# Following each batch read of sample states with one adaLN unit in a hybrid GLA and Mamba-2 decoder step

## The chip, the cores and the metric

The kernel runs on one core of a Trainium2 chip. The metric is the device time of one execution in microseconds: 2923.5 us, the median of three runs (2923.2 to 2926.08).

## The reference

One decoder layer for 256 prompt tokens and 8 sequences of 8 sample tokens (320 token columns), in float32. The vector `c` of each sequence gives six adaLN parts of 2048 values; they scale, shift and gate the two halves of the layer.

```
mod  = silu(c) @ w_ada + b_ada                 # 9 rows of c; w_ada is 2048 x 12288
h    = rmsnorm(x) * (1 + sc1) + sh1
proj = h @ w_in
# GLA, 4 heads:  S_t = diag(a_t) S_{t-1} + k_t^T v_t ,  o_t = q_t S_t
# SSD, 64 heads in 8 groups:  h_t = exp(dt_t A) h_{t-1} + dt_t x_t B_t^T ,  y_t = h_t C_t
x = x + g1 * ((sigmoid(gA) * yA + sigmoid(gB) * yB) @ w_mix_out)
x = x + g2 * SwiGLU(rmsnorm(x) * (1 + sc2) + sh2)
y = rmsnorm(x) * final_norm
```

The sample sequences start from stored states (8 sequences x 4 heads x 256 x 512 for GLA; 8 x 64 heads x 64 x 128 for SSD), which are read, updated and written back.

## The kernel before

**Weights.** All large products run as "quads": `quad_mm` (L318) takes a 512 x 512 block of a weight matrix in two halves. A half is one transfer of 128 x 1024 float32 (524,288 bytes) into a buffer with the tag `raw`, of which there are four (`load_raw`, L160). ScalarE casts it to `whi` and VectorE makes the rest `wlo` (`split_w`); of these pairs there are three. TensorE then runs 24 matmuls of 128 x 320 per half (`block`, L312: three per 128 x 128 tile). `Stream.ahead` (L190) asks for the half two further on each time the first of a half's four column blocks is done. TensorE's order is that of the program; the other engines and SyncE's queue (SP), which issues every transfer, are ordered by the compiler's scheduler, in program order as far as buffers and data allow. `now(...)` says that a transfer is placed no earlier in that order than the TensorE instruction before it.

**adaLN units.** `class Ada` (L242) cuts `w_ada` into units. A unit of the later kind is a 128 x 2048 block: two raw transfers (`load`, L253) and four matmuls with 32 columns of stationary each, put side by side in TensorE at column positions 0, 32, 64 and 96 (`mm`, L275); in float32 they run as eight passes. After each fourth unit the sums are copied out (`adap`, L291), and at the next call of `mm` the `flush` (L294) transposes that copy (four matmuls `p`) and writes the strips of `mod`. 96 units there are; 64 are left when the GLA part starts, and four of them are kept for the end of the mixing stage. Between, `gemm` (L352) puts one unit into each quad whose number divides by `ada_every`: its load at the start of the quad, its matmuls at the end. `ada_every` is 0 through the GLA heads and 2 from L926 to the end of the units, so 60 units go there.

**States.** Beside the quads runs a background: `bg.tick()` is called after each of a quad's eight column blocks (a tick is six matmuls), and a generator's `yield n` lets n ticks pass, so that it goes on at the one after those. `gla_work` (L640) and `ssd_work` (L963) handle the sample states as 128 x 512 tiles (262,144 bytes, ten buffers). `States.read` (L617) loads ahead to tile 4n + 8 and then runs four matmuls of the same shape as an adaLN unit, 32 columns each at positions 0 to 96, as eight passes named `inter`. `States.update` (L624) runs one matmul `upd`, changes one tile and stores the one before. A GLA head has four reads, an SSD group two: 32 in all. In a GLA head the first read comes at tick 18 of the head's work (24 in the first head) and the others each 10 ticks later; in an SSD group at ticks 16 and 26. Behind the first read of an SSD group two tiles `csb` of 655,360 bytes each are loaded (L1003). `bg.drain()` runs what is left of the background at once, with no quads beside it; the first head has eight quads, 64 ticks, before it.

Of the kernel before, what the change touches and what calls it, by code (L numbers as in the profile page):

```python
# [60 lines left out]
def hybrid_kernel(tc, ctx, a, o):  # L61
# [186 lines left out]
    class Ada:  # L248
# [12 lines left out]
        def load(self, small=False, spare=False):  # L261
            if self.units:
# [8 lines left out]
                    raws = [load_raw(src[:, h * 1024:(h + 1) * 1024], spare or c < 8) for h in range(2)]  # L271
                self.loaded.append((c, b0, nb, q, raws))

        def mm(self):
            self.flush()  # L275
            if not self.loaded:
                return
            c, b0, nb, q, raws = self.loaded.pop(0)
            if q == 0:
                t = psum.tile([128, 512], F32, tag="ad", bufs=1, name="ad")  # L280
                self.ps = t
            w = 128 * nb
            m = 2048 // w
            n = m // len(raws)
            for j in range(m):
                T.matmul(self.ps[32 * (j % 4):32 * (j % 4) + 32, :w], c_s[:, m * q + j, :],
                         raws[j // n][:, (j % n) * w:(j % n) * w + w], start=q == 0 and j < 4,
                         stop=q == nb - 1 and j >= m - 4, tile_position=(0, 32 * (j % 4)))
            if q == nb - 1:
                part = stile([128, 512], name="adap")  # L290
                S.copy(part[:, :w], self.ps[:, :w])  # L291
                self.parts.append((c, b0, nb, part))
# [59 lines left out]
    def gemm(names, quads, evac, apart=False):  # L352
        pss = [mm_ps() for _ in range(4)]
        n = len(names)
        for q in range(n):
            quad_no[0] += 1
            xq = quads(q) if callable(quads) else quads[q]
            quad_mm(pss, names[q], xq, q == 0, q == n - 1, evac,
                    1 if ada_every[0] and len(ada.units) > 4 and quad_no[0] % ada_every[0] == 0 else 0, apart,
                    (lambda: quads(q + 1)) if callable(quads) and q + 1 < n else None)  # L360


# [149 lines left out]
    def stack_k(ps, hf, n):  # L512

        R = pool.tile([96, n, 128], F32R, tag="k", bufs=3, name="R")
        src = ps[quarter(hf), 0:128 * n].rearrange("p (a b) -> p a b", a=n)
        S.copy(R[quarter(0)], src)
        S.copy(R[quarter(1)], src)
        tt(V, R[quarter(2)], src, R[quarter(hf)].bitcast(F32), ALU.subtract)
        return [stack_stationary(R[:, i]) for i in range(n)]
# [120 lines left out]
    def gla_work(H):  # L640
        hd, vT, KK, qe, kx = H.hd, H.vT, H.KK, H.qe, H.kx
        order = [(4 * hf + j, kb) for hf in range(2) for kb in range(2) for j in range(4)]
        states = States([a["S_gla"][hd, b, kb] for b, kb in order], [o["gla_s"][hd, b, kb] for b, kb in order])
        yield 6 if hd else 12
        states.load(4)
        yield 4


        psK = ax_ps("kT")
        for kb in range(2):  # L650
            T.transpose(psK[0:64, 128 * kb:128 * kb + 128], kx[:, kb, 0:64], ident)
        ps = ax_ps("vT")
        for mb in range(4):
            T.transpose(ps[0:64, 128 * mb:128 * mb + 128], vT[:, mb, NP:], ident)
        S.copy(xs_tok[0:64], ps[0:64])
        hst = [stack_k(psK, hf, 2) for hf in range(2)]
        yield 4

        psA = ax_ps("inter")
        for n in range(4):  # L660
            hf, kb = divmod(n, 2)
            if kb == 0:
                mv = stack_v(xs_tok, hf)
            states.read(psA, [H.qpad[:, kb, 4 * hf + j] for j in range(4)], n, n == 0, n == 3)
            yield 1
            for j in range(4):
                tok = NP + 8 * (4 * hf + j) + 7

                def decay(st, ps, kb=kb, tok=tok):
                    V.scalar_tensor_tensor(out=st, in0=st, scalar=H.eb[:, kb, tok:tok + 1], in1=ps,  # L670
                                           op0=ALU.mult, op1=ALU.add)

                states.update(n, j, hst[hf][kb][:, j], mv, decay)
                yield 1
        inter = stile([128, 512], name="inter")
        S.copy(inter, psA)
        yield 1
        states.store(16)
        vt = []
        for tb in range(2):  # L680
            ps = ax_ps("vT")
            for mb in range(4):
                T.transpose(ps[:, 128 * mb:128 * mb + 128], vT[:, mb, 128 * tb:128 * tb + 128], ident)
            v = stile([128, 512], name="vtok")
            S.copy(v, ps)
            vt.append(v)
            yield

        att = stile([128, 448], name="att")
        now(G.memset(att, 0.0))  # L690
        ps = ax_ps("att")
        for i in range(4):
            for kb in range(2):
                T.matmul(ps[:, 64 * i:64 * i + 64], KK[kb][:, 256 * i:256 * i + 128],
                         qe[:, kb, 64 * i:64 * i + 64], start=kb == 0, stop=kb == 1)
        yield
        for i in (2, 3):
            for kb in range(2):
                T.matmul(ps[:, 128 + 64 * i:192 + 64 * i], KK[kb][:, 256 * i + 128:256 * i + 256],
                         qe[:, kb, 64 * i:64 * i + 64], start=kb == 0, stop=kb == 1)  # L700
        for kb in range(2):
            T.matmul(ps[0:64, 384:448], H.kes[:, kb], qe[:, kb, NP:], start=kb == 0, stop=kb == 1)
        V.copy_predicated(att[:, 0:384], mask[:, 0:384].bitcast(I32), ps[:, 0:384])
        V.copy_predicated(att[0:64, 384:448], mask[0:64, 384:448].bitcast(I32), ps[0:64, 384:448])
        yield

        k4 = stile([128, 2, 256], name="k4")
        for sb in range(2):
            ps = ax_ps("k4")
            for kb in range(2):  # L710
                T.transpose(ps[:, 128 * kb:128 * kb + 128], KK[kb][:, 1024 + 128 * sb:1152 + 128 * sb], ident)
            S.copy(k4[:, sb], ps[:, 0:256])
            yield

        oT = qtile(name="oT")
        ss = ntile([128, NT], name="ss")
        for mb in range(4):
            c = slice(128 * mb, 128 * mb + 128)
            ps = ax_ps("o")
            T.matmul(ps[:, 0:256], vt[0][:, c], att[:, 0:256], start=True, stop=False)  # L720
            T.matmul(ps[:, 128:256], vt[1][:, c], att[:, 256:384], start=False, stop=True)
            T.matmul(ps[:, 256:320], xs_tok[0:64, c], att[0:64, 384:448], start=True, stop=False)
            T.matmul(ps[:, 256:320], inter[:, c], sel, start=False, stop=True)
            S.copy(oT[:, mb], ps[:, :NT])
            sq_acc(ss, oT[:, mb], mb == 0, G)
            yield
        yield 4
        while H.r is None:
            yield
        rs = rstd_from([ss], 512)  # L730
        H.hi = qtile(F32R, name="ohi")
        H.lo = qtile(F32R, name="olo")
        for mb in range(4):
            V.scalar_tensor_tensor(out=oT[:, mb], in0=oT[:, mb], scalar=vec[:, V_GN + mb:V_GN + mb + 1],
                                   in1=rs, op0=ALU.mult, op1=ALU.mult)
            tt(G, oT[:, mb], oT[:, mb], H.r[:, mb], ALU.mult)
            split(H.hi[:, mb], H.lo[:, mb], oT[:, mb])
        for kb in range(2):
            ps = ax_ps("fin")
            for sb in range(2):  # L740
                T.matmul(ps, k4[:, sb, 128 * kb:128 * kb + 128], vt[sb], start=sb == 0, stop=sb == 1)
                yield
            fs = stile([128, 512], name="fs")
            S.copy(fs, ps)
            nc.sync.dma_start(o["gla_p"][hd, kb], fs)
# [177 lines left out]
    prev = heads[3]  # L923


    ada_every[0] = 2  # L926

    def conv_evac(ck, dst, cvs, cvo):
        def f(mb, pss):
# [40 lines left out]
    def ssd_work(W):  # L970
# [19 lines left out]
        xl = stile([64, 512], name="xl")  # L990
        tt(V, v8(xl), v8(ps[0:64]), bc8(dtL_tok[:, hsl]), ALU.mult)
        tt(V, v8(xs_tok[0:64]), v8(ps[0:64]), bc8(dt_tok[0:64, 2, hsl]), ALU.mult)
        yield 4

        psA = ax_ps("inter")
        for hf in range(2):
            mv = stack_v(xl, hf)
            states.read(psA, [cpad[:, 4 * hf + j] for j in range(4)], hf, hf == 0, hf == 1)
            for j in range(4):
                st = states.tiles[4 * hf + j]  # L1000
                tt(G, v8(st), v8(st), bc8(ecs_all[:, hsl, 4 * hf + j]), ALU.mult)
# [8 lines left out]
            yield 1  # L1010
            for j in range(4):
                states.update(hf, j, hst[hf][:, j], mv, lambda st, ps: tt(V, st, st, ps, ALU.add))
                yield 1
        inter = stile([128, 512], name="inter")
        tt(V, v8(inter), v8(psA), bc8(ecs_r[:, hsl]), ALU.mult)
# [418 lines left out]
```

## Time and profile before

| what | value |
|---|---|
| median of three runs | 2923.5 us |
| the profiled execution | 2922.56 us |
| its span, first to last instruction | 2920.8 us |
| mean granted TensorE clock | 0.995 of full speed |
| TensorE busy (matmul) | 2874.5 us, 98% |
| VectorE, ScalarE, GpSimd busy | 54%, 42%, 13% |
| moved by DMA | 575.54 MB, mean 197 GB/s |

In the page, PE is TensorE's matmuls and PEld its weight loads, DVE is VectorE, ACT ScalarE, POOL GpSimd and SP the queue that issues the transfers. The GLA part lies at about 185 to 610 us, the SSD groups at about 610 to 1655 us.

### The profile page before, as it was taken

What the parts mean: (1) busy time and instruction counts of PE and PEld (TensorE: products, weight loads), DVE (VectorE), ACT (ScalarE), POOL (GpSimd) and SP (SyncE); (2) the same over time, 40 slices, a digit from 0 to 9 for tenths busy, and PEclk for the clock granted to TensorE, in tenths of its full rate; (3) what the DMA queues carried; (4) which work ended last, traced back from release to release, by engine and by line L of the source; (5) the groups of instructions that cost most, each with busy time, mean ns of one, the idle gap of its engine ahead of it and who ended that gap; (6) DMA issues with size and microseconds to landing.
All of it is one profiled execution on the core that took longest, in us unless ns stands there. A gap on an engine that the chain in (4) does not pass through costs nothing.

```text
span 2920.8 us, 48446 instructions
## 1 busy us (share of the span) xinstructions
PE 2874.5 (98%) x19596; PEld 2687.3 (92%) x19596; DVE 1584.6 (54%) x2302; ACT 1239.1 (42%) x1954; POOL 375.5 (13%) x517
## 2 busy tenths in 40 slices
PE   7999999999999999999999999999999999999998
PEld 5799788998889889889988999999999999999998
DVE  5666555756656565666565554456434444444445
ACT  4344544343554554545454343335333233323333
POOL 0002121212232232323223000000000000000000
PEclk9999999999999999999999999999999999999998
DMA  9847636657676675775757554454444444444443
GB/s 385 321 146 238 202 126 215 220 177 264 221 245 232 228 254 191 253 237 206 265 194 253 195 170 161 165 211 145 152 151 148 149 152 152 147 149 152 151 147 114
DMA packets 181112, 575.54 MB, mean 197 GB/s; under 512 B 23253, under 2 KB 24601, under 8 KB 180889
## 3 DMA queue, kind: packets, MB, share of 16 engines
q1 hardware_dynamic: 180888, 572.45, 57.5%
q8 instruction: 154, 2.52, 0.3%
q14 instruction: 70, 0.57, 0.1%
HBM read 528.63 MB, written 43.74 MB: 196 GB/s over the span
## 4 chain that ended last, share of the span: by engine, by line
PE 55%; DVE 1%; ACT 0%; issue 0%; DVEq 0%
PE mm L115 52%; PE ad L115 1%; PE y L115 0%; DVE x L106 0%; PE sum L115 0%; PE upd L115 0%; PE fin L115 0%; PE inter L115 0%; DVE x L1182 0%; PE p L118 0%; PE cb L115 0%; PE xT L118 0%; DVE ss L106 0%; DVE wlo L106 0%; DVE yb L106 0%
## 5 line engine op out<-in xcount | busy, mean ns | idle before, releaser
L106 DVE TENSOR_TENSOR wlo<-raw,whi 128x1024 fp32r<-128x1024 f32 x712 | 881.4, 1240 | 933.9 <-ACT whi L132 923.4
L132 ACT CAST whi<-raw 128x1024 fp32r<-128x1024 f32 x712 | 745.8, 1048 | 1384.8 <-PE mm L115 1040.6
L115 PE MATMUL mm<-hh,whi 128*128 128x320 f32 x2560 | 813.2, 318 | 2.4 <-ACT hh L132 2.0
L115 PE MATMUL mm<-hl,whi 128*128 128x320 f32 x2560 | 791.0, 309 | 1.3 <-DVE hl L106 1.3
L115 PE MATMUL mm<-hh,wlo 128*128 128x320 f32 x2560 | 791.7, 309 | 0.1
L115 PEld LDWEIGHTS mm<-hh,whi 128*128 128x128 f32 x2560 | 481.3, 188 | 81.3 <-issue 37.3
L115 PEld LDWEIGHTS mm<-hl,whi 128*128 128x128 f32 x2560 | 481.7, 188 | 10.1 <-issue 2.9
L115 PEld LDWEIGHTS mm<-hh,wlo 128*128 128x128 f32 x2560 | 481.5, 188 | 0.6 <-DVE wlo L106 0.4
L115 PE MATMUL mm<-gh,whi 128*128 128x320 f32 x1408 | 435.3, 309 | 0.8 <-ACT gh L1256 0.8
L115 PE MATMUL mm<-gl,whi 128*128 128x320 f32 x1408 | 435.4, 309 | 0.0
L115 PE MATMUL mm<-gh,wlo 128*128 128x320 f32 x1408 | 435.1, 309 | 0.0
L115 PEld LDWEIGHTS mm<-gh,whi 128*128 128x128 f32 x1408 | 264.3, 188 | 1.8 <-ACT gh L1256 1.8
L115 PEld LDWEIGHTS mm<-gl,whi 128*128 128x128 f32 x1408 | 264.3, 188 | 0.5 <-DVE gl L106 0.3
L115 PEld LDWEIGHTS mm<-gh,wlo 128*128 128x128 f32 x1408 | 264.3, 188 | 0.0
L115 PE MATMUL mm<-ahi,whi 128*128 128x320 f32 x704 | 217.5, 309 | 0.0
L115 PE MATMUL mm<-alo,whi 128*128 128x320 f32 x704 | 217.5, 309 | 0.0
L115 PE MATMUL mm<-ahi,wlo 128*128 128x320 f32 x704 | 217.5, 309 | 0.0
L106 POOL TENSOR_TENSOR ss<-ss,sq 128x320 f32<-128x320 f32 x14 | 12.4, 883 | 1398.0 <-ACT sq L109 1397.9
L115 PE MATMUL mm<-yhi,whi 128*128 128x320 f32 x512 | 170.4, 333 | 0.1
L115 PE MATMUL mm<-yhi,wlo 128*128 128x320 f32 x512 | 158.4, 309 | 0.2 <-DVE wlo L106 0.2
L115 PE MATMUL mm<-ylo,whi 128*128 128x320 f32 x512 | 158.0, 309 | 0.0
L115 PEld LDWEIGHTS mm<-ahi,whi 128*128 128x128 f32 x704 | 132.1, 188 | 0.0
(281 smaller groups left out, 3624.6 us busy)
## 6 DMA issues: line engine op xcount, KB each, us to landing
raw<-w_in SPq DMA_DIRECT2D x320, 512.0 KB, 3.8
raw<-w_fi SPq DMA_DIRECT2D x176, 512.0 KB, 3.6
raw<-w_ada SPq DMA_DIRECT2D x120, 512.0 KB, 5.7
raw<-w_fo SPq DMA_DIRECT2D x88, 512.0 KB, 3.5
raw<-w_sp SPq DMA_DIRECT2D x64, 512.0 KB, 5.0
araw<-w_ada SPq DMA_DIRECT2D x52, 512.0 KB, 8.9
st<-S_gla SPq DMA_DIRECT2D x64, 256.0 KB, 5.1
gla_s<-st SPq DMA_DIRECT2D x64, 256.0 KB, 4.7
```

Of the source, the lines that this page charges most:

```text
L106: return eng.tensor_tensor(out=out, in0=in0, in1=in1, op=op)
L115: Tensor.last = nc.tensor.matmul(*args, **kw)
L132: first = S.copy(hi, src)
```

## The change

Reads and units are coupled. `Ada.unit` is the old `mm` without the flush in front. `Ada.preload` loads one unit if none is waiting. In the background each `states.read` is followed at once by `ada.unit()`, and the next unit's load is issued there or, for the first read, five ticks before it. The flush moves behind the first update after each read. `ada_every` goes from 2 to 4, a quad takes no unit while one is loaded, and the GLA heads' ticks change: the first pause is 2 instead of 6 (not in the first head), and the pause after the first update of each four is 2 instead of 1. So the reads of a GLA head come at ticks 14, 25, 36 and 47 (24, 35, 46 and 57 in the first head).

```diff
+        def preload(self):
+            if len(self.units) > 4 and not self.loaded:
+                self.load()
+
         def mm(self):
             self.flush()
+            self.unit()
+
+        def unit(self):
             if not self.loaded:
                 return
...
-                    1 if ada_every[0] and len(ada.units) > 4 and quad_no[0] % ada_every[0] == 0 else 0, apart,
+                    1 if ada_every[0] and len(ada.units) > 4 and quad_no[0] % ada_every[0] == 0 and not ada.loaded else 0, apart,
...
-        yield 6 if hd else 12
+        yield 2 if hd else 12
...
         hst = [stack_k(psK, hf, 2) for hf in range(2)]
+        ada.preload()
         yield 4
...
             states.read(psA, [H.qpad[:, kb, 4 * hf + j] for j in range(4)], n, n == 0, n == 3)
+            ada.unit()
+            if n < 3:
+                ada.preload()
             yield 1
...
                 states.update(n, j, hst[hf][kb][:, j], mv, decay)
-                yield 1
+                if j == 0:
+                    ada.flush()
+                yield 2 if j == 0 else 1
...
-    ada_every[0] = 2
+    ada_every[0] = 4
...
         tt(V, v8(xs_tok[0:64]), v8(ps[0:64]), bc8(dt_tok[0:64, 2, hsl]), ALU.mult)
+        ada.preload()
         yield 4
...
             states.read(psA, [cpad[:, 4 * hf + j] for j in range(4)], hf, hf == 0, hf == 1)
+            ada.unit()
+            if hf == 0:
+                ada.preload()
...
                 states.update(hf, j, hst[hf][:, j], mv, lambda st, ps: tt(V, st, st, ps, ALU.add))
+                if j == 0:
+                    ada.flush()
                 yield 1
```

## Rows read from the trace of the kernel before

**Rows 1.** The page's first part: busy time and share of each engine.
```profile
PE 2874.5 (98%) x19596; PEld 2687.3 (92%) x19596; DVE 1584.6 (54%) x2302; ACT 1239.1 (42%) x1954; POOL 375.5 (13%) x517
```

**Rows 2.** The chain in order of time: start us, us, what, passes.
```profile
1426.37 1.00 PE inter L115 x8
1427.36 0.86 PE ad L115 x8
1428.22 1.95 PE mm L115 x12
1430.41 1.76 PE mm L115 x12
...
1445.36 0.99 PE ad L115 x8
1446.35 1.95 PE mm L115 x12
...
1532.28 1.00 PE inter L115 x8
1533.27 0.59 PE p L118 x4
1533.86 0.99 PE ad L115 x8
```

**Rows 3.** Groups by line on TensorE, whole span: xcount | busy us, mean ns | idle before.
```profile
L115 PE MATMUL ad<-raw,c_s 128*32 128x512 f32 x480 | 63.8, 604 | 0.0
...
L115 PE MATMUL inter<-st,cpad 128*32 128x512 f32 x128 | 17.0, 605 | 0.0
```

**Rows 4.** Stretches: us, busy of PE PEld DVE ACT POOL, PEclk, DMA share, GB/s.
```profile
640.00:1655.00 1015.00, 1012.49 (x7053) 906.78 (x7051) 635.27 (x910) 498.64 (x932) 289.68 (x398) 1.00 0.68 231
683.00:693.00 10.00, 10.00 (x72) 8.86 (x70) 5.32 (x8) 4.04 (x8) 2.39 (x3) 1.00 0.63 213
693.00:713.00 20.00, 20.00 (x133) 16.41 (x132) 14.05 (x16) 6.35 (x10) 10.30 (x8) 1.00 0.95 341
240.00:274.00 34.00, 34.00 (x227) 29.38 (x225) 21.12 (x22) 12.18 (x15) 2.61 (x3) 1.00 0.88 295
285.00:310.00 25.00, 20.84 (x106) 15.36 (x106) 10.09 (x13) 11.37 (x23) 6.90 (x7) 0.93 0.18 67
```

**Rows 5.** Timeline of the issuing queue in the first SSD group.
```profile
692.44 1.85 SPq L619 DMA_DIRECT2D st<-S_ssm  x4
694.33 1.11 SPq L1008 DMA_DIRECT2D csb<-cs_d  x2
695.54 0.47 SPq L167 DMA_DIRECT2D raw<-w_in  x1
...
700.42 0.38 SPq L167 DMA_DIRECT2D raw<-w_ada  x1
...
701.42 0.51 SPq L167 DMA_DIRECT2D raw<-w_ada  x1
```

**Rows 6.** Timeline: split and first use of a half behind csb, two SSD groups.
```profile
704.86 1.05 ACT L132 CAST whi<-raw 128x1024 fp32r<-128x1024 f32 x1 [7.29 <-DMA raw<-w_in]
705.95 1.53 DVE L106 TENSOR_TENSOR wlo<-raw,whi 128x1024 fp32r<-128x1024 f32 x1 [2.64 <-ACT whi L132]
707.60 0.34 PE L115 MATMUL mm<-hh,wlo 128*128 128x320 f32 x1
...
1057.32 1.23 DVE L106 TENSOR_TENSOR wlo<-raw,whi 128x1024 fp32r<-128x1024 f32 x1 [1.23 <-ACT whi L132]
1060.04 0.31 PE L115 MATMUL mm<-hh,wlo 128*128 128x320 f32 x1
```

**Rows 7.** Timeline: split and first use of a half in the first GLA head.
```profile
255.02 1.23 DVE L106 TENSOR_TENSOR wlo<-raw,whi 128x1024 fp32r<-128x1024 f32 x1
263.37 0.31 PE L115 MATMUL mm<-hh,wlo 128*128 128x320 f32 x1
```

**Rows 8.** The tile ad: the copy on ScalarE, ns min/median/max.
```profile
L291 ACT COPY adap<-ad x26: 372/583/602, 20.9 to 1972.4; 128x512 f32<-128x512 f32 x22, 128x256 f32<-128x256 f32 x4
```

## The prediction

> **What bounds the kernel now.** I began with the page's busy shares: TensorE's matmuls fill 98% of the span and no other engine comes near [rows 1]. A table of stretches confirms it where the change works: in the SSD part, 640 to 1655 us, matmuls are busy 1012.49 of 1015 us at granted clock 1.00, the higher level, 2.4 GHz [rows 4]. So only less TensorE time per piece of work helps there, and the price of every new wait is paid in full.
>
> Next I read the chain in order of time for what a change of shape costs. Twelve steady weight matmuls take 1.76 us; the twelve behind an adaLN unit take 1.95. A unit alone (0.99) with its aftermath (0.19) thus costs 1.18 us, and a read, of the same shape, as much. Where a read and a unit stand together, the chain has 1.00, then 0.86, then 1.95 for twelve: 2.05 us for both, against 2 x 1.18 = 2.36 apart. **A pair saves 0.31 us** [rows 2].
>
> Last I looked at how early weights arrive, in the timelines. In the first GLA head a half's split ends at 256.25 (255.02 + 1.23) and is first used at 263.37, 7.1 us later [rows 7]. In the SSD groups the half whose transfer is issued behind the two csb loads is much tighter: in the first group ScalarE waits 7.29 us for it, the split ends at 707.48 and the first use is at 707.60, 0.1 us later; in another group it is 1058.55 and 1060.04, 1.5 us [rows 6]. I count four groups of the first kind and four of the second. The reserve is small there because the transfers are: the DMA engines are 0.95 busy at 341 GB/s from 693 to 713 us, though only 0.63 in the ten microseconds before [rows 4].
>
> **The change part by part.**
>
> *The pairs.* The 480 passes under `raw` are 60 units of eight, and the 128 passes of `inter` in the SSD groups are 16 reads of eight [rows 3]; the GLA heads have 16 more. Four units go to each GLA head and two to each SSD group, so all 32 reads get one, and 28 units stay in quads. By the ticks every preload finds none waiting: the quad numbers divisible by four are the last of each group of four quads, and the one in an SSD group's z product is left out, since a unit is loaded then. The slots suffice for the 28. Eight of the 32 reads are followed by a unit already: four directly (the last at 1426.37), four with a flush between (the last at 1532.28). The 24 new pairs save 24 x 0.31 = 7.4 us. In the other four the flush moves away: 1.00 + 0.59 + 0.99 + 0.19 = 2.77 becomes 2.05 and a flush of at most 0.59, so 0.13 to 0.31 each; I take 0.22, 0.9 us [rows 2]. Together **-8.3 us**, between -7.9 and -8.6.
>
> *The flushes.* Their number stays; eight of them now come two ticks (some 2 us) after their unit. The copy takes 0.58 us on ScalarE [rows 8], and a cast of 1.05 us [rows 6] can stand ahead of it: 1.6 us, so it fits and I take nothing. If a cast that waits for its weights stands ahead, TensorE waits with it; at 1 us each that would be 8 us, which I keep for the upper end.
>
> *The first GLA head.* Its updates now end at tick 66 of 64, so one falls into the drain. The stretch of that drain has matmuls busy 20.84 of 25 us [rows 4], there is nothing to hide behind. One `upd` and its store: 0.3 us, bounds 0 and 2. **+0.3 us**. The other heads end at the same tick as before (4 earlier at the start, one more for each of four reads).
>
> *Transfers in the GLA heads.* Sixteen units' loads of 1.05 MB move here, three of them in each head between the first read and the last, which lie 33 ticks, some 38 us, apart. The stretch now moves 295 GB/s at a share of 0.88, so 335 at a share of 1 [rows 4]. With the reads 11 ticks apart instead of 10 this thins to 268; three units in 38 us add 83: 351 against 335. That is 5% too much for 38 us, 1.8 us late per head at most if nothing absorbs it, against a reserve of 7.1 [rows 7]. But a waiting unit holds two of the four raw buffers nearly throughout, so the weights run less far ahead, and the next unit's load can block the queue until the present unit has run; behind it stand state loads, stores and weights. Bounds 0 and 7.2 us for four heads; nearest is the reserve, so I take 0.25 per head: **+1.0 us**.
>
> *Transfers in the SSD groups.* This decides. The second unit of a group is now loaded behind the first read (693 us in the first group); before, its two transfers went out at 700.42 and 701.42, behind the csb loads and the weights issued at 695.54 [rows 5]. It comes ahead of them, and its 1.05 MB at 341 GB/s are 3.1 us [rows 4]. Had the queue no room, each tight group would lose 3.0 us and each other 1.6. The room is in the stretch before, 0.37 of 10 us idle [rows 4], enough for 3.7 us; but a load starts only when a raw buffer comes free, and the order of the buffers lets one of the two transfers go early (the weights' half that stood behind the first unit's load now goes before it, is split earlier and frees its buffer), while the other waits for the first unit's matmuls. So half of the 3.1 us, 1.5, meets the full stretch: 1.4 in the four tight groups, nothing in the others. **+5.6 us**; bounds -2.5 (what TensorE now idles in the whole part, by the 1012.49 of 1015) and 4 x 3.0 + 4 x 1.6 = 18.4. The later load of the same kind, two quads on, is gone, so nothing is late a second time.
>
> The Trainium skill, DMA: Bandwidth & Descriptors, "Specifications", gives 435 GB/s as the fabric's ceiling and about 358 for a core's share of HBM. By the 435 the half unit would take 1.2 us, the GLA heads would lose nothing and the sum would be -3.6; the rows' 341 at a share of 0.95 speak for the lower figure.
>
> *Sum:* -8.3 + 0.3 + 1.0 + 5.6 = -1.4 us on the profiled execution's 2922.56, 2921.2. That execution lies 0.9 us below the median of the runs, so 2922.1 on the median's scale.
>
> **The rivals.**
>
> *All loads hide (chance 0.33).* The unit's transfers use the idle time ahead of the full stretch altogether. For it: DMA share 0.63 before it, the GLA reserve of 7.1 us, and fewer units in the quads around it. Against: two of four raw buffers are held by the unit before. Then -8.3 + 0.3 = -8.0, **2915.5**.
>
> *The second unit's load delays the weights whole (0.20).* Place: SP's queue behind the first read of every SSD group. If both transfers, or a state load stuck behind the one that waits for its buffer, stand ahead of the csb loads and the weights, TensorE waits at the half after next: 4 x 3.0 + 4 x 1.6 = 18.4 us, so -8.3 + 0.3 + 1.0 + 18.4 = +11.4, **2934.9, slower**. From (8.3 - 0.3 - 1.0) / 8 = 0.9 us of new waiting per group on the saving is gone, from 1.6 us on the kernel is slower by more than 0.2%. For it: the reserve of 0.1 us and the 7.29 us that ScalarE waits already [rows 6]. Against: the room before. The Trainium skill, DMA: Bandwidth & Descriptors, "Queues, rings and completion order", says that each DMA engine takes descriptors in ring order; by that rule weights issued later cannot pass the unit, and the rows on the late half agree.
>
> *The GLA heads' transfers run full (0.08).* All of the 7.2 us is paid, and the SSD part as forecast: -8.3 + 0.3 + 7.2 + 5.6 = +4.8, **2928.3**.
>
> *The pairs don't form (0.03).* If the unit waits for its own data behind the read, TensorE idles and the saving is spent: the old time, **2923.5**.
>
> **How the numbers follow.** My forecast has 0.36; its own range is 2917 to 2928. About 0.2%, 5.85 us, is what a measurement of this kernel can tell from no change: below 2917.65 is faster, above 2929.35 slower. Faster: 0.33 of the first rival and 0.02 of the forecast, 0.35. Slower: 0.20 of the second, 0.04 of the third and 0.04 of the forecast, 0.28. The rest, 0.37, is no change that can be told. The range, 2914.5 to 2936, holds the first rival with its bound and the second's time; a second rival with slow flushes on top is left out.
>
> **What would show it.** Right: 32 groups of `inter` followed by `ad` on the chain, 0.86 for the second; a wait of 1 to 2 us at one half in each of four SSD groups, with ScalarE waiting for `raw` before it; GLA heads without gaps. First rival: busy share in the SSD part unchanged or higher, all of the saving there. Second: a gap of 2 to 3 us in every SSD group, always at the half issued behind csb. The prediction is wrong at its root if a unit next to a read costs much more than 0.86.

## The result and the profile after: 84 us slower

The changed kernel takes **3007.95 us** (median of four runs, 3004.68 to 3008.42) against 2923.57 of the kernel before: a ratio of 1.028, 95% interval 1.0265 to 1.0295. The profiled execution took 3008.28 us, its span is 3006.5 us, the mean granted clock 0.982 (0.995 before). It moves the same bytes and runs the same 19596 passes, so all of the 84 us is waiting or slower work.

Ahead of any chain I look at the waits of TensorE (engine, line, what it waited for: us in total, times, longest us). In the kernel before, its weight matmuls waited for weights once, for 0.2 us:

```profile
PE mm L115 <- DVE wlo L106: 0.2, 1, 0.2
```

Now, first in the whole span, then from 640 to 1740 us, the SSD groups, then from 200 to 640 us, the GLA heads:

```profile
PE mm L115 <- ACT whi L132: 50.1, 15, 6.4
PE mm L115 <- DVE wlo L106: 8.2, 16, 0.7
...
PE mm L115 <- ACT whi L132: 39.1, 8, 6.4
PE mm L115 <- DVE wlo L106: 2.9, 8, 0.4
...
PE mm L115 <- ACT whi L132: 11.0, 7, 3.7
PE mm L115 <- DVE wlo L106: 5.4, 8, 0.7
```

58.3 us of waiting for weights: 42.0 in the SSD groups, one wait for `whi` and one for `wlo` in each of the eight, together 4.5 to 6.8 us in a group, and 16.4 in the GLA heads. The place is the one that [rows 6] showed to be tight, the first half issued behind `csb`, but the loss is in all eight groups and not in four.

The chain in order of time tells what the late half waited for, in the first SSD group (start us, us, what):

```profile
736.62 1.24 DVE wlo L106
...
737.87 0.33 SPq L167
...
738.25 0.42 SPq L626
...
740.14 0.49 SPq L1025
...
741.24 8.86 DMA raw<-w_in
...
750.20 1.05 ACT whi L132
...
751.27 1.24 DVE wlo L106
```

Read it from the end. TensorE waits for the split; the split waits for the transfer; the transfer was asked for at 741.24. Ahead of that the queue itself is on the chain: two `csb`, four `st`, and one L167, which is the second transfer of the unit. That one stood until 737.87, when VectorE had split an earlier half and so freed a raw buffer. In the timeline of the queue the unit's two transfers are one entry of 6.42 us; the first went out at 731.79 and took 0.33 us to issue, so the second stood for some 5.7 us:

```profile
729.27 0.33 SPq L167 DMA_DIRECT2D raw<-w_in  x1
731.79 6.42 SPq L167 DMA_DIRECT2D raw<-w_ada  x2
738.25 1.85 SPq L626 DMA_DIRECT2D st<-S_ssm  x4
...
741.24 1.79 SPq L167 DMA_DIRECT2D raw<-w_in  x2
```

In the kernel before, the line ahead of those of [rows 5] is

```profile
692.06 0.33 SPq L167 DMA_DIRECT2D raw<-w_in  x1
```

Against the first state read on TensorE (691.52 us before, 736.49 now) the state loads go out 0.9 us later before and 1.8 us later now, so this group of transfers has hardly moved. What has moved is one half of weights. Counted from the start of the kernel, 143 halves were issued ahead of the first `csb` loads and now 142 are; in each of the eight groups it is one less. The half that went out 0.5 us behind the read (692.06) now goes out 4.75 us behind it, on the other side of the four states and the two `csb`. ScalarE took it up 4.5 us after its issue before (696.52), and takes it up 9.0 us after its issue now (750.20), after 12.32 us of waiting for it. The unit's two transfers have the place and the buffers that this half had.

What a wait costs beyond itself is in TensorE's timeline and in the stretches around it (columns as in [rows 4]):

```profile
751.29 0.64 PE L115 MATMUL mm<-hh,whi 128*128 128x320 f32 x1 [4.69 <-ACT whi L132]
...
752.55 0.64 PE L115 MATMUL mm<-hh,wlo 128*128 128x320 f32 x1 [0.36 <-DVE wlo L106]
752.98 0.47 PE L115 MATMUL mm<-hh,whi 128*128 128x320 f32 x1
753.25 0.47 PE L115 MATMUL mm<-hl,whi 128*128 128x320 f32 x1
```

```profile
732.00:742.00 10.00, 10.00 (x72) 8.32 (x71) 5.38 (x7) 3.52 (x5) 5.42 (x5) 1.00 0.63 193
...
752.00:757.00 5.00, 4.64 (x23) 3.08 (x26) 1.72 (x2) 1.50 (x2) 0.02 (x1) 0.58 0.60 197
```

TensorE idles 4.69 us, and then its granted clock is 0.58 for five us, mostly the lower level, 1.2 GHz: a matmul starts each 0.27 us and not each 0.147 (12 in 1.76 us, [rows 2]). Those five us hold 23 passes where ten us before held 72, 36 in five: 13 passes, 1.8 us, most of it on top of the 5.1 us of waiting. The Trainium skill, TensorE: Matmul & The Clock Gate, section "Part 1: The HAM clock gate", says that an idle TensorE is put at half rate; the 0.58 agrees.

The GLA heads show the other form. Here a half goes out only when one before it has been split. The chain of the first head, and TensorE's waits at its end:

```profile
243.09 1.24 DVE wlo L106
...
244.34 0.33 SPq L167
...
244.77 6.07 DMA raw<-w_in
...
250.86 1.05 ACT whi L132
...
251.94 1.24 DVE wlo L106
```

```profile
251.96 0.42 PE L115 MATMUL mm<-hh,whi 128*128 128x320 f32 x1 [1.48 <-ACT whi L132]
...
253.22 0.41 PE L115 MATMUL mm<-hh,wlo 128*128 128x320 f32 x1 [0.70 <-DVE wlo L106]
```

A split frees a buffer, the unit's transfer that waited for it goes first (L167, 244.34), then the half; it takes 6.07 us to land and 2.3 to split, and TensorE waits 1.48 and 0.70 us. The half of [rows 7] was split 7.1 us ahead of its use; this reserve is gone. The unit has two of the four buffers from one read to the next.

### The profile page after: what moved, and what is told of

It is laid out like the page before. It is cut to its first block, busy times and chain, and to the rows that moved or that the text cites. A ratio compares the mean times of both kernels' runs of the same rounds, so it can differ in the third digit from the quotient of the medians.

```text
span 3006.5 us, 48400 instructions
## 1 busy us (share of the span) xinstructions
PE 2903.2 (97%) x19596; PEld 2711.7 (90%) x19596; DVE 1580.1 (53%) x2302; ACT 1241.3 (41%) x1954; POOL 377.0 (13%) x517
## 4 chain that ended last, share of the span: by engine, by line
PE 86%; DMA 6%; DVE 3%; ACT 2%; SPq 1%; issue 1%; POOL 0%; ACTq 0%; DVEq 0%; POOLq 0%
PE mm L115 77%; DMA raw<-w_in 6%; PE ad L115 2%; DVE wlo L106 1%; ACT whi L132 1%; PE y L115 1%; PE inter L115 1%; PE fin L115 1%; PE o L115 1%; PE upd L115 1%; ACT w L109 1%; PE sum L115 1%; SPq L626 0%; PE att L115 0%; POOL w L106 0%
## 5 line engine op out<-in xcount | busy, mean ns | idle before, releaser
L115 PE MATMUL mm<-hh,whi 128*128 128x320 f32 x2560 | 823.1, 322 | 53.1 <-ACT whi L132 50.1
L115 PE MATMUL mm<-hh,wlo 128*128 128x320 f32 x2560 | 801.4, 313 | 8.4 <-DVE wlo L106 8.2
L115 PEld LDWEIGHTS mm<-hh,whi 128*128 128x128 f32 x2560 | 487.6, 190 | 131.0 <-ACT whi L132 62.7
L115 PEld LDWEIGHTS mm<-hh,wlo 128*128 128x128 f32 x2560 | 487.9, 191 | 14.0 <-DVE wlo L106 14.0
L115 PEld LDWEIGHTS mm<-hl,whi 128*128 128x128 f32 x2560 | 488.6, 191 | 8.8 <-issue 2.9
```

What stands on the lines that cost most here:

```text
L115: Tensor.last = nc.tensor.matmul(*args, **kw)
```

## The experiments

Each diff is against the changed kernel unless it says otherwise. A kernel that ran once is compared with the kernel before on the same chip. That kernel lay between 2919 and 2935 us over all chips, and on one chip its executions were up to 14 us apart, so a difference of a few us against a single run is not told from none. I had two theories. A: the units' transfers take raw buffers from the weights and block the queue, so halves are asked for late. B: they are too many bytes where they now are. A third, C, was that reads, units and ticks cost time by themselves.

**No transfers.** The 32 coupled units load nothing and multiply by a tile that is there anyway:

```diff
-                self.load()
+                src, c, b0, nb, q = self.units.pop(0)
+                self.loaded.append((c, b0, nb, q, [c_s.rearrange("p a b -> p (a b)")] * 4))
```

> The 32 units beside reads run their matmuls on a resident tile and issue no transfer (their weights are left out); order, ticks and pairs stay those of the change. If the 84 us come from the units' transfers and the buffers they hold (theories A, buffers and order, and B, bytes), only the pairs' saving is left: about 2915 us, no weight half late. If the pairs or the new ticks themselves cost (theory C), it stays near 3000.

2915.61 us, against 2925.84 of the kernel before: 10.2 less, where the change with its transfers was 84 more. C falls. The pairs cost what the prediction said, in the chain:

```profile
706.53 1.00 PE inter L115 x8
707.53 0.86 PE ad L115 x8
708.39 1.95 PE mm L115 x12
```

This run also divides the loss. Its span is 2913.8 us with TensorE busy 2868.9, so 44.9 idle; the changed kernel, busy 2903.2 of 3006.5, has 103.3 idle. Of the 92.7 us between the two spans 58.4 are waits, the 58.3 of the first view, and 34.3 are matmuls that took longer, at a mean clock of 0.982 against 0.994. The clock is enough to explain them: busy time times clock is 2851 us in one and 2852 in the other.

**Half the bytes.** The same buffers at the same places, with half of the columns transferred:

```diff
-                self.load()
+                for h in range(2):
+                    raw = stage.tile([128, 1024], F32, tag="raw", bufs=4, name="raw")
+                    nc.sync.dma_start(raw[:, 0:512], src[:, h * 1024:h * 1024 + 512])
+                    raws += [raw, raw]
```

> The same 32 units load only half of their columns (0.52 instead of 1.05 MB per unit; half of their weights are left out), but hold the same two raw buffers, issued at the same place. Theory A (a weight half is late because the unit's tiles take the buffers it would have had, so that it is requested late and stands behind state and csb loads): most of the loss stays, 2975 to 2995 us. Theory B (too many bytes in the stretch): the loss halves, about 2955 to 2965.

2970.06 us: 54 above the run without transfers where the full bytes gave 92. Between the two theories; waits for weights are 32.5 us (24.9 and 7.6) where they were 58.3. Fewer bytes land sooner and let buffers go sooner, so this run alone decides nothing.

**The SSD load later.** The second unit of a group is loaded behind the first update, so behind `csb` and the weights:

```diff
             ada.unit()
-            if hf == 0:
-                ada.preload()
...
                 if j == 0:
                     ada.flush()
+                    if hf == 0:
+                        ada.preload()
```

> Only the place of the second preload in an SSD group changes: behind the first update instead of behind the first read, so that one weight half is asked for before it. The bytes stay. Theory A: the SSD part's 57 us fall to 15 or less, the GLA part's 28 stay: 2945 to 2965 us. Theory B: no change, about 3005.

2954.54 us, 53 less for a move of two ticks with every byte kept. This is for A in the SSD groups.

**GLA heads alone, SSD groups alone.** In the first the SSD part is as before (`ada_every` 2, no coupled units); in the second the GLA part is.

> The GLA heads as changed, the SSD groups as before (units in every second quad until they run out). If the losses of the two parts are independent, as the trace has them (28 us in the GLA heads, 57 in the SSD groups): about 2951 us. If the GLA part's stalls come with the SSD part's density or the order as a whole, it differs by over 10 us.

> The changed kernel in the SSD groups alone: the GLA heads as before, without units and with their old pauses; the 16 units not used there go into every second quad behind the last SSD group. If the two halves of the loss are independent, this has the SSD part's loss alone: 2923 plus 57 to 66, 2980 to 2990 us. If the GLA heads only hand their delay on, it is nearer to 3008.

2943.95 us against 2925.84, and 2990.7 against 2927.05: 18 and 64, together 82 of the 84. By these two runs the losses of the two parts add up.

**A fifth raw buffer**, and its control on the kernel before:

```diff
-N_S = 10
-N_ST = 10
+N_S = 9
+N_ST = 9
...
-            raw = stage.tile([128, 1024], F32, tag="raw", bufs=4, name="raw")
+            raw = stage.tile([128, 1024], F32, tag="raw", bufs=5, name="raw")
```

> The changed kernel with five raw buffers in place of four (paid for with nine state and nine s buffers in place of ten). Theory A (the unit's two transfers take raw buffers from the weights and block the issuing queue until one comes free): the late half can be asked for in time, most of the waits go, 2935 to 2965 us. Theory B (the bytes of the unit are too many where they are put): the same bytes in the same places, 2990 to 3010.

> The kernel before with the same buffers (five raw, nine state, nine s): the control for the run above. Both theories: 2920 to 2930 us; what it lies above the kernel before is the price of the smaller rings.

2930.83 and 2926.2 us, with the kernel before at 2922.44. Bytes and places are those of the change, and 76 of its 84 us are gone. Of the remaining 8.4 the control has 3.8, by one run each, which is too little to be told. B falls as a cause by itself. The queue in the first SSD group of the changed kernel with five buffers:

```profile
711.57 2.85 SPq L167 DMA_DIRECT2D raw<-w_ada  x2
717.60 0.33 SPq L167 DMA_DIRECT2D raw<-w_in  x1
717.98 1.85 SPq L626 DMA_DIRECT2D st<-S_ssm  x4
719.87 0.92 SPq L1025 DMA_DIRECT2D csb<-cs_d  x2
720.89 0.48 SPq L167 DMA_DIRECT2D raw<-w_in  x1
```

The unit is through in 2.85 us and not 6.42, and the half that had lost its place stands ahead of the state loads again, the 143rd; it is so in all eight groups. The Trainium skill, DMA: Bandwidth & Descriptors, "Queues, rings and completion order", has each DMA engine take its descriptors in ring order; the late half, which takes 8.86 us behind states and `csb` where it took some 4.5 ahead of them, agrees with it. That is one half of the delay: measured from the read, this half lands 8.7 us later than before. The other half, 4.2 us, arises before the ring, where the half is issued late.

**Other buffers for the units.** `self.load(True)` in `preload`: four tiles of 128x512 of the tag `s`, each with a transfer of its own in `now(...)`, which the plain `load` of these units does not have.

> The changed kernel with the 32 coupled units loaded into four buffers of 128x512 of the tag s instead of two raw ones: place in the queue and bytes unchanged, all four raw buffers stay with the weights. Theory A: 2920 to 2940 us, if the s buffers are free when they are asked for. Theory B: 2985 to 3010. A value between, 2945 to 2975, would say that a third to a half of the loss is the place in the queue and not the buffers.

2977.66 us, and neither theory's number: the condition was not met. No weight matmul waits for weights any more, but the units wait for their own data (waits of TensorE, and a unit of the first SSD group):

```profile
PE ad L115 <- DMA araw<-w_ada: 24.4, 24, 2.6
```

```profile
746.38 3.08 PE L115 MATMUL ad<-araw,c_s 128*32 128x512 f32 x8 [1.10 <-DMA araw<-w_ada]
```

Waits of 24.4 us are not all: a unit's eight passes last 3.08 us here, and the span is 61.8 us above that of the run without transfers, 24.4 of these waits and 37.5 of longer busy time, in the units' passes. The place in the queue did change, against what I expected: the first unit of this group goes out at 726.50 in the changed kernel, 10.0 us ahead of its read, and here at 739.91, 4.3 us ahead, which fits the `now`, and lands 6.43 us later. So buffers and place changed together, and this run does not say which of them made the loss. The queues of the changed kernel and of this run:

```profile
726.50 2.00 SPq L167 DMA_DIRECT2D raw<-w_ada  x2
```

```profile
739.91 1.85 SPq L268 DMA_DIRECT2D araw<-w_ada  x4
```

The mean clock stayed at 0.995 in this run.

**GLA heads alone, loads later.** Against the run with the GLA heads alone (by the pauses it is five ticks, not the four that I wrote):

```diff
             ada.unit()
-            if n < 3:
-                ada.preload()
...
+                if j == 1 and n < 3:
+                    ada.preload()
```

> As the run with the change in the GLA heads alone (2943.95 us), but the next unit is loaded behind the second update after a read, four ticks later, instead of right behind the read: the two raw buffers are held for some 8 us of every 13 instead of nearly always. Theory A: the waits in the heads shrink with that, 2925 to 2936 us. Theory B: the bytes per head are the same, 2940 to 2946.

2930.21 us: 14 less, waits for weights 1.6 us in place of 15.8. This is for A in the heads as well.

**Both later loads together.**

> The changed kernel with both later placings together: in the SSD groups the second unit is loaded behind the first update, in the GLA heads each next one behind the second update after a read. Theory A: the two gains add, 2954.5 less 13.7 is 2941 us, between 2936 and 2946. Theory B: the bytes are unchanged, 2950 or more.

2929.96 us, better than the sum: 78 of the 84 us are undone by moving two calls. What is left of the waits for weights is 2.9 us.

**No transfer moved, reads moved to the units.** On the kernel before, the second SSD read goes to the end of the fourth quad, and a unit runs ahead of the flush; the second run also gives the reads of all GLA heads but the first a unit each. The diff of the first:

```diff
-                yield 1
+                yield 7 if hf == 0 and j == 3 else 1
...
-            ada.mm()
+            ada.mm_late()
```

> The kernel before with no transfer moved: the second read of an SSD group goes from tick 26 to tick 32, where a unit already stands at the end of the quad, and a quad's unit runs ahead of the flush instead of behind it, so that all 16 SSD reads are followed by a unit. Eight new pairs at 0.31 us and four flushes moved away at 0.22: 3.4 us less than the kernel before, 2919 to 2921.5, if pairs save what the rows said and the transfers made the loss. If a pair costs something else, 2923 or more.

> The run before this one, and in the GLA heads but the first 12 reads each with a unit, loaded behind the second update after the read before. By the run with late loads in the GLA heads, whose last three heads came out 1.4 us ahead: 2917.5 to 2921. By the pairs alone, 12 more at 0.31 us: 2916. If units in the GLA heads still take weights' buffers, 2921 or more.

2959.1 us (1.0108, 1.0091 to 1.0125) and 2957.21 (1.0103, 1.0085 to 1.0121): both missed by 35 us or more. Six ticks later at the second read are six ticks later for all that follows, and a group's norm falls into the convolutions of the next. In the profiled execution of the first kernel, the slowest of its four, TensorE waits 24.5 us for `wlo`, with the raw data long there. The timelines of ScalarE, VectorE and TensorE, at one of these waits:

```profile
785.10 1.08 ACT L132 CAST whi<-raw 128x1024 fp32r<-128x1024 f32 x1
```

```profile
787.29 0.82 DVE L949 TENSOR_SCALAR cacc<-u,vec 128x344 f32<-128x344 f32 x2
...
792.14 3.00 DVE L952 SCALAR_TENSOR_TENSOR cacc<-u,vec,cacc 128x344 f32<-128x344 f32 x6
795.06 2.35 DVE L106 TENSOR_TENSOR wlo<-raw,whi 128x1024 fp32r<-128x1024 f32 x2
```

```profile
796.33 0.63 PE L115 MATMUL mm<-hh,wlo 128*128 128x320 f32 x1 [3.90 <-DVE wlo L106]
```

ScalarE's cast was done at 786.18, VectorE made `wlo` of it from 795.06 on, behind 7.8 us of `cacc`. VectorE has an order, too, and by this trace it was fuller at the new place; no run tested that.

**What was left.** With both later loads the kernel was still some 14 us above the run without transfers. Four kernels with both later loads pay for a fifth raw buffer in different ways: nine state and nine `s`; eight state; nine `s`, three `w` and four `n` buffers; three `w` and three `n`.

> Both later placings and the fifth raw buffer (nine state and nine s buffers). The control with these buffers was 3.8 us slower than the kernel before, and the pairs save 8. If what was left of the loss with both later placings (some 12 us above the run without transfers) is still the buffers, the pairs show: 2916 to 2922 us. If it is VectorE's order at the group's end or the bytes, it stays: 2926 to 2934.

> The same with the fifth raw buffer paid for by two state buffers (eight) and none of the s buffers. If the smaller s ring made the control slow, this is 3 to 5 us faster than the run with nine and nine, 2914 to 2919 us; if the state ring did, it is slower than that run, since eight hold no tile ahead.

> Both later placings and the fifth raw buffer, paid for by one s buffer, one of the w buffers of the SSD decay weights and one of the small n buffers; the ten state buffers stay. If the state ring is what costs the run with nine and nine its 9 us in the GLA heads, 2915 to 2920 us, faster than the kernel before by what the pairs save; if the s ring is, 2923 to 2928.

> The same, but paid for by one w buffer and two n buffers, with all ten s and ten state buffers. If the s ring costs the GLA heads their time, this is the faster of the two, 2915 to 2920 us; if three n buffers are too few for the gates and norms, 2925 or more.

Nine and nine: 2925.92 us, 0.9998 (0.9986 to 1.001). Eight state buffers: 2943.66, 1.0056 (1.0041 to 1.0071), where the reads wait for states:

```profile
PE inter L115 <- DMA st<-S_gla: 12.6, 8, 2.9
```

With all ten state buffers kept: **2918.11 us, 0.9975 (0.9963 to 0.9986)** and 2919.69, 0.9981 (0.9971 to 0.9991). It was the state ring that cost the GLA heads their time: behind them, the first `xs` of the SSD part (L1115) is made at 761.2 us with nine state buffers and at 753.1 with ten, both with nine `s`. No wait for weights is left in the faster of the two, and its SSD part, 625 to 1655 us, is full (columns as in [rows 4]):

```profile
625.00:1655.00 1030.00, 1029.61 (x7152) 947.82 (x7152) 654.06 (x916) 520.19 (x957) 309.99 (x407) 1.00 0.62 213
```

Two controls with the same buffers, the kernel before and the changed kernel as it is:

> The kernel before with the buffers of the fastest run (five raw, nine s, three w, four n): the control for it. If the pairs are what made that run faster, this stays at the kernel before, 2921 to 2927 us; if the fifth raw buffer alone did, it comes out at 2916 to 2920.

> The changed kernel as it is, loads right behind the reads, with these buffers. By the run with nine state and nine s buffers (2930.8), whose rings cost the GLA heads 9 us: 2920 to 2925, as fast as the kernel before. If the early loads still cost something with five buffers, it is 3 us or more above the run with later loads (2918).

2921.53 us, 0.9988 (0.9979 to 0.9997), and 2924.21, 0.9997 (0.9989 to 1.0006). So of the 6.4 us by which the fastest kernel beats the one before about half, 3, comes from the buffers and the other half from the coupled units with later loads. The intervals of the two steps overlap, though no run of the fastest kernel (2915.98 to 2919.82) is as long as any of the control (2919.92 to 2923.1); they ran on two chips, so the second half is likely and not certain. The change as written, given the buffer it needs, breaks even with the kernel before as it is; against that kernel with the same buffers, on the same chip, it is still 2.7 us slower.

## Why the prediction was wrong, point by point

*What bounds the kernel.* Right: TensorE, with nothing to spare, so that each new wait was paid in full.

*The pairs, -8.3.* Right, as far as single runs tell. A pair is 1.86 us and a slower start of the next twelve (1.95), as forecast, and with the transfers away the kernel gained 10.2 by one pair of runs, 7.0 by the spans of two traces (2920.8 and 2913.8); -8.0 with the drain was forecast.

*The flushes, 0.* Right: TensorE's waits for `adap` are 1.0 us in two places, in both kernels.

*The first head's drain, +0.3.* Too small. From the first instruction without quads to the first projection matmul it took 20.7 us and takes 23.4 (TensorE's timelines, before and after; the third line of each is the end of it, and the second one of its longer pieces):

```profile
283.78 1.04 PE L118 MATMUL vT<-erl,col 128*128 128x128 f32 x8
...
297.25 5.29 PE L115 MATMUL fin<-vtok,k 128*128 128x512 f32 x8
...
304.48 0.41 PE L115 MATMUL mm<-olo,whi 128*128 128x320 f32 x1 [0.43 <-DVE olo L106]
```

```profile
295.76 0.63 PE L115 MATMUL upd<-mv,hs 96*128 96x512 f32 x2
...
311.07 6.00 PE L115 MATMUL fin<-vtok,k 128*128 128x512 f32 x8
...
319.17 0.53 PE L115 MATMUL mm<-olo,whi 128*128 128x320 f32 x1 [0.65 <-DVE olo L106]
```

I had counted one `upd` and its store; two stand there, 0.5 us, and `vT` comes in two parts behind them, 0.6 us more. Over 1 us is the clock, which no term had: it was 0.92 from 283 to 304 us and is 0.86 from 295 to 319, and `sum` and `fin` are longer by 0.6 and 0.7 us. The run without transfers has the same 23.4 us, so this cost is the order's and not the loads'.

*Transfers in the GLA heads, +1.0.* Wrong by a factor of about twenty: 18 us lost by the heads alone and 5 saved by their 16 pairs (16 x 0.31) make 23, of which 2.7 are the drain above; the trace has 16.4 us of waits for weights. The sentence that a waiting unit "holds two of the four raw buffers nearly throughout" named the cause; the step that failed is the next one, "nearest is the reserve, so I take 0.25 per head". The reserve of [rows 7] was what four buffers give; with two it does not exist. Even the upper end, 7.2, was worked out from bytes alone.

*Transfers in the SSD groups, +5.6.* Wrong by a factor of more than ten: 42.0 us of waits, and with the clock 64 lost by these groups alone beside the 3.4 that their pairs save. The failed step is "the order of the buffers lets one of the two transfers go early", while the other waits: I priced the other's bytes, half of 3.1 us. The rows show two things in its place. The second transfer waited 5.7 us for a split and not for the first unit's matmuls, and the queue stood still behind it. And the two took the buffers and the place of one half of weights, which so went out behind the states and `csb`: measured from the read, 4.2 us later than before, and it landed 8.7 us later. The bounds fell with it: 18.4 was 3.0 and 1.6 us per group for bytes that stand ahead.

*The rivals.* The second, "the second unit's load delays the weights whole", had the place, the queue, the half behind `csb` and even the state load stuck behind the one without a buffer. Its price was the same 3.0 and 1.6, from bytes. The rows have 4.5 to 6.8 us of waits in a group, in all eight, 5.2 in the mean.

*What no part had.* The clock: 34.3 us of the loss are matmuls that ran longer; in the rows shown they stand behind a wait, at the lower level. Every new wait was priced at its length, where the whole span has 34.3 us of slower work to 58.4 of waiting: together 1.6 times the waiting.

## What to carry to other kernels

Before moving a load earlier, count what buffer it needs, who holds that buffer at the new place and for how long, and what stands behind it in the same queue: a load without a buffer stops all loads behind it, and the price is the time by which those come later, not its bytes alone. Count also which load loses its buffer to it, and behind what that one then stands. A prefetch belongs behind the transfers that are due sooner, just early enough for its own use; here a few ticks at two places were worth 78 us. Where one ring is shared by two streams, one more buffer can be worth as much as a better order (76 us and 78 here), but take it from a ring whose tiles nobody waits for.

## What the runs showed of the hardware that I had not expected

A wait of 4.69 us is followed by some four us at 1.2 GHz, an estimate from the clock of 0.58 over five us (a matmul each 0.27 us). In the run with late loads in the GLA heads alone the clock falls in a drain: behind the first head TensorE idled 1.47 us until 290.51, waiting for `vtok`, and the stretch from 300 to 318 us ran at 0.65, below full speed for most of it:

```profile
300.00:318.00 18.00, 14.08 (x36) 8.55 (x35) 7.11 (x7) 6.84 (x13) 6.82 (x7) 0.65 0.10 37
```

The whole run waited for weights 1.6 us. In the kernel before, where this drain lies some ten us earlier, 285 to 300 us had 0.93 and 300 to 318 us 0.96. In the run with both later loads the same drain has 1.00 and 0.81; why the other fell lower was not tried. And 24.4 us of waits in 24 pieces, the longest 2.6 us, in the run with `s` buffers left the mean clock at 0.995.
